# A decoder trunk on one core: GpSimd scales three pieces of the turned input, the compressed attention branch works on block-diagonal operands, and the split of the turned FFN hidden is placed later

## The chip, the cores and the metric

The kernel runs on one core of one Trainium2 chip. The metric is the device time of one execution in microseconds (us). The kernel before was timed three times: 1020.0, 1019.18 and 1019.8 us, median 1019.8 us. A separate execution was profiled.

## The reference

Two layers, each a half-step SwiGLU, a token mixer and another half-step SwiGLU; then a last norm. There are 256 rows of 1024 channels, the hidden width of the SwiGLU is 2816, and all is float32.

```python
for l in range(DEPTH):                       # 2
    x = x + 0.5 * swiglu(rms_norm(x, norm_ffn1[l]), gate1[l], up1[l], down1[l])
    x = x + hybrid_mixer(rms_norm(x, norm_mix[l]), w_in[l], ..., w_out[l])
    x = x + 0.5 * swiglu(rms_norm(x, norm_ffn2[l]), gate2[l], up2[l], down2[l])
return rms_norm(x, norm_final)

def swiglu(x, w_gate, w_up, w_down):
    return (silu(x @ w_gate) * (x @ w_up)) @ w_down
```

The mixer has four groups of four heads. Only one branch of one group matters here, the compressed branch of the sparse attention: keys and values of 256 rows are squeezed into 15 blocks each by a small network (`compress`), and each of the four query heads attends to the same 15 keys and values:

```python
kc, vc = compress(k_cmp, 0), compress(v_cmp, 1)          # 15 blocks x 64
s_cmp = einsum('bhtd,bnd->bhtn', q, kc) * scale - slopes * cmp_dist
p_cmp = masked_softmax(s_cmp, cmp_dist >= 0)
o_cmp = einsum('bhtn,bnd->bhtd', p_cmp, vc)              # times a gate, added to two other branches
```

## The kernel before, in words

**Halves and sets.** The 256 rows are two halves, h = 0 and h = 1, of 128 rows each. All large weights come as *sets* of 512 KB (`Set`, L123; a 128x2x512 tile). SyncE's queue loads a set into one of four `raw` buffers (L137); `split` (L119 to L121) then makes a high part `whi`, a copy on ScalarE, and a low part `wlo`, raw minus high, on VectorE. A product of set and half is six matmuls on TensorE (`Set.mm`, L149): two blocks of 128 rows, each high x high, high x low, low x high. The activations are split in the same way: `xhi` and `xlo` for the normed input, `hhi` and `hlo` for the hidden of the SwiGLU. Since all splits go through `split`, the trace books them under L115, the line in `keep` that issues them; the tile's name tells them apart.

**Order of the work.** The program walks over the sets (`consume`, L748): half 0 uses set i, half 1 uses set i - 5 (`LAG`), and loads run two sets ahead (`AHEAD`). After each use, `advance` (L179) moves all waiting jobs on by one step, so that a job which yields n is taken up again n uses later. No order is written out by hand beyond this: each engine runs its instructions in the order in which the framework has placed them. `tc.issue_after(ins)` places what is issued in it behind `ins`.

**The feed-forward blocks** (`add_ffn`, L281). There are four, each of 11 chunks of 256 hidden columns. A chunk is four gate/up sets (accumulator `ps_g`) and two down sets (`ps_d`); the down sets of chunk c stand behind the gate/up sets of chunk c + 2. Behind the last gate/up set, `gate_up` (L311) makes the hidden `sg` on ScalarE and VectorE (L318, L319). The hidden must be turned before the down product. In chunks 0, 1 and 10 TensorE does so (`turn`, L286). In the eight others (`turn_far`, L294), VectorE transposes 32x32 blocks (`z`, L298), GpSimd's queue writes them to DRAM in four pieces (`far<-z`, L301), reads them back four steps later (`pT<-far`, L305), and ten steps after that the split into `hhi` and `hlo` is issued (L309). Chunks 2 to 9 of a block are called far chunks below.

**The start** (`begin`, L717). The first block takes its input already turned from DRAM in four pieces: two for each half (`take_turned`, L237). VectorE multiplies each piece by the norm's weight `gcol` (L249), and the split follows. The first piece is cut in two parts of 128x256, the other three are 128x512. The order of the start is fixed by `keep` (L111), which puts every operation of VectorE and ScalarE behind the one before it. TensorE is kept busy by products with `idle`, a tile that VectorE zeroes (L96, L101).

**The compressed branch in the mixer.** `compress` (L482) loads the first layer's weights in four pieces into `raw` buffers and runs eight matmuls behind each (L497), so they stand between the products of the sets; the second layer gives `kc` (L517, the 64 x 15 keys, held twice in the 128 partitions) and `vc` (L519, 15 x 64). `cmp_branch` (L523) then uses `attend` (L429) as all branches do: four score products of a 64-row contraction (L399), a softmax (L402), a multiplication by the weight for each head (L437), four transposes (L445), a copy of 15x512 on ScalarE (L448), and four value products (L457), for each half and layer.

## Time and profile before

| | |
|---|---|
| three runs | 1020.0, 1019.18, 1019.8 us (median 1019.8) |
| the profiled execution's own time | 1020.97 us |
| its span, first to last instruction | 1019.2 us |
| granted TensorE clock, mean over the span | 0.995 |
| TensorE (PE) busy | 996.3 us, 98% |
| VectorE (DVE) busy | 642.0 us, 63% |
| ScalarE (ACT) busy | 515.8 us, 51% |
| GpSimd (POOL) busy | 195.0 us, 19% |
| mean DMA rate over the span | 197 GB/s |

A row of the timeline has the start of an operation, its duration and, in brackets, how long its engine stood idle before it and which event ended that. PE is TensorE, PEld its weight loads, which run beside its matmuls. TensorE's matmuls overlap: each 512-column product shows as some 0.39 us, though the next one starts earlier, so its pace is read from starts, not from durations. Idle time of an engine that nobody waits for costs nothing.

### The profile page before, as it was taken

The page shows a single profiled execution, that of the slowest core. Times are in us where ns is not written, and L with a number is a line of the kernel's source. Part 1 is how long each engine was busy: PE and PEld are TensorE (multiplying, and loading weights), DVE is VectorE, ACT ScalarE, POOL GpSimd, SP SyncE. Part 2 cuts the span into 40 slices and gives each one's busy share as a digit, 9 for nine tenths or more (in the row PEclk, how much of TensorE's full clock was granted, in tenths as well). Part 3 has the DMA queues.
Part 4 walks back from the last instruction along what each step waited for, and adds up shares of the span by engine and source line. Part 5 has one row for each costly group of instructions (what it writes and reads, how often), then busy time and mean ns, then how long its engine had stood idle before and what let it go on. Part 6 is the DMA issues. An engine that isn't in the chain of part 4 may idle for free.

```text
span 1019.2 us, 14178 instructions
## 1 busy us (share of the span) xinstructions
PE 996.3 (98%) x4899; PEld 801.4 (79%) x4899; DVE 642.0 (63%) x1223; ACT 515.8 (51%) x886; POOL 195.0 (19%) x351
## 2 busy tenths in 40 slices
PE   8999999999999999999999999999999999999997
PEld 5788787867778888788878888878678788888875
DVE  6565656786777456465755565648776775656464
ACT  6444444554665445354644454446466564445452
POOL 0132323010000023332102232310100001323230
PEclk9999999999999999999999999999999999999999
DMA  8677767644354466676656777755634455677671
GB/s 294 235 224 262 235 220 244 207 151 166 119 166 139 154 212 215 219 221 237 204 175 202 222 229 224 235 186 176 189 109 155 128 166 190 205 234 214 220 232 47
DMA packets 68855, 200.36 MB, mean 197 GB/s; under 512 B 12448, under 2 KB 20528, under 8 KB 68784
## 3 DMA queue, kind: packets, MB, share of 16 engines
q1 hardware_dynamic: 56352, 180.83, 55.1%
q0 software_dynamic: 11712, 17.86, 5.4%
q8 instruction: 38, 0.62, 0.3%
q10 hardware_dynamic: 720, 0.79, 0.2%
q14 instruction: 33, 0.27, 0.1%
HBM read 189.98 MB, written 9.45 MB: 196 GB/s over the span
## 4 chain that ended last, share of the span: by engine, by line
PE 40%; DMA 26%; DVE 11%; POOL 9%; issue 7%; ACT 7%; POOLq 0%; SPq 0%; ACTq 0%; DVEq 0%
PE ps_g L149 22%; DMA far<-z 13%; DMA pT<-far 11%; PE ps_d L149 10%; POOL far L301 9%; DVE wlo L115 5%; ACT whi L115 4%; PE ps_t L457 2%; DVE sg L319 2%; DMA wraw<-in_gu 1%; PE ps_t L445 1%; DVE z L298 1%; PE ps_d L399 1%; PE ps_t L379 1%; PE ps_t L262 1%
## 5 line engine op out<-in xcount | busy, mean ns | idle before, releaser
L115 DVE TENSOR_TENSOR wlo<-wraw,whi 128x1024 fp32r<-128x1024 f32 (+3 forms) x329 | 392.4, 1196 | 176.6 <-ACT whi L115 175.6
L115 ACT ACTIVATE whi<-wraw 128x1024 fp32r<-128x1024 f32 (+3 forms) x329 | 341.0, 1038 | 224.9 <-PE ps_g L149 105.4
L149 PE MATMUL ps_g<-whi,xhi 128*128 128x512 f32 (+2 forms) x896 | 352.0, 394 | 5.8 <-ACT whi L115 3.8
L149 PE MATMUL ps_g<-wlo,xhi 128*128 128x512 f32 (+2 forms) x896 | 347.5, 388 | 3.7 <-DVE wlo L115 3.6
L149 PE MATMUL ps_g<-whi,xlo 128*128 128x512 f32 (+2 forms) x896 | 346.4, 387 | 0.0
L149 PEld LDWEIGHTS ps_g<-whi,xhi 128*128 128x128 f32 x896 | 168.6, 188 | 47.5 <-ACT whi L115 6.7
L301 POOL DMA_DIRECT2D far<-z x256 | 139.8, 554 | 327.4 <-DVE z L298 322.8
L149 PEld LDWEIGHTS ps_g<-wlo,xhi 128*128 128x128 f32 x896 | 168.7, 188 | 37.3 <-DVE wlo L115 6.8
L149 PEld LDWEIGHTS ps_g<-whi,xlo 128*128 128x128 f32 x896 | 168.5, 188 | 31.7 <-DVE xlo L115 0.5
L149 PE MATMUL ps_d<-whi,hhi 128*128 128x512 f32 x352 | 138.9, 395 | 0.0
L149 PE MATMUL ps_d<-whi,hlo 128*128 128x512 f32 x352 | 137.8, 391 | 0.0
L149 PE MATMUL ps_d<-wlo,hhi 128*128 128x512 f32 x352 | 137.6, 391 | 0.0
L115 ACT ACTIVATE hhi<-pT 128x256 fp32r<-128x256 f32 x64 | 26.7, 417 | 153.4 <-DMA pT<-far 153.4
L115 DVE TENSOR_TENSOR hlo<-pT,hhi 128x256 fp32r<-128x256 f32 x64 | 27.2, 425 | 107.5 <-ACT hhi L115 107.4
L149 PEld LDWEIGHTS ps_d<-whi,hlo 128*128 128x128 f32 x352 | 66.4, 189 | 13.9
L149 PEld LDWEIGHTS ps_d<-wlo,hhi 128*128 128x128 f32 x352 | 66.6, 189 | 13.6
L149 PEld LDWEIGHTS ps_d<-whi,hhi 128*128 128x128 f32 x352 | 66.5, 189 | 13.4
L159 POOL TENSOR_TENSOR rstd<-ms,mhalf 128x1 f32<-128x1 f32 x14 | 8.6, 614 | 291.4 <-DVE ms L157 291.4
L305 POOL DMA_DIRECT2D pT<-far x64 | 35.6, 557 | 142.4 <-DMA far<-z 111.9
L318 ACT ACTIVATE sg<-ps_g,rstd 128x256 f32<-128x256 f32 x88 | 41.1, 467 | 22.4 <-PE ps_g L149 22.1
L319 DVE SCALAR_TENSOR_TENSOR sg<-ps_g,rstd,sg 128x256 f32<-128x256 f32 x88 | 42.1, 478 | 15.8 <-ACT sg L318 15.8
L416 ACT ACTIVATE p<-p,nm 128x128 f32<-128x128 f32 (+2 forms) x96 | 40.1, 419 | 22.8 <-DVE nm L408 10.5
(158 smaller groups left out, 654.4 us busy)
## 6 DMA issues: line engine op xcount, KB each, us to landing
wraw<-in_gu SPq DMA_DIRECT2D x175, 512.0 KB, 4.1
wraw<-in_down SPq DMA_DIRECT2D x88, 512.0 KB, 4.5
wraw<-in_win SPq DMA_DIRECT2D x24, 512.0 KB, 4.0
far<-z POOLq DMA_DIRECT2D x256, 32.0 KB, 4.0
pT<-far POOLq DMA_DIRECT2D x64, 128.0 KB, 3.7
wraw<-in_wout SPq DMA_DIRECT2D x16, 512.0 KB, 3.5
wraw<-in_win SPq DMA_DIRECT2D x16, 384.0 KB, 3.6
wraw<-in_w SPq DMA_DIRECT2D x8, 512.0 KB, 3.5
```

Source lines behind the costliest of these rows:

```text
L115: ins = f(*args, **kw)
L149: nc.tensor.matmul(acc, x_[k], w[:, k, :], start=first and i == 0, stop=last and i == 5)
L262: nc.tensor.transpose(pt[:, j, :], xg[:, j * P:(j + 1) * P], ident)
L298: nc.vector.transpose(st, hh)
L301: nc.gpsimd.dma_start(far[:, :, a_, :].rearrange("b j e -> j b e"), st[32 * a_:32 * a_ + 32].rearrange("j (b e) -> j b e", b=4))
L305: nc.gpsimd.dma_start(back, far.rearrange("b j a e -> (b j) (a e)"))
L318: nc.scalar.activation(sg, acc[h][:, :256], AF.Silu, scale=r)
L319: nc.vector.scalar_tensor_tensor(sg, acc[h][:, 256:], r, sg, op0=ALU.mult, op1=ALU.mult)
L379: nc.tensor.transpose(pt[:, j, :], z[:, j * P:(j + 1) * P], ident)
L399: nc.tensor.matmul(dst, qT[r, i // 2, :], keys(i)[r, :nk], start=True, stop=True)
L416: nc.scalar.activation(p[:, i, :], p[:, i, :], AF.Exp, bias=nm[:, i:i + 1], scale=-1.0, accum_out=den[:, i:i + 1])
L457: nc.tensor.matmul(o[64 * e:64 * e + 64, j, :], vals(2 * j + e, n), pts[n][:w, 2 * j + e, :], start=n == 0, stop=n == len(blocks) - 1)
```

## The change

In order of the program:

- A constant tile `pc` (128x4x32) is zeroed once on GpSimd; the warm-up products read the zeroed tile `ph` instead of `idle`, whose memset on VectorE goes.
- In `take_turned` the three 128x512 pieces are multiplied by `gcol` on GpSimd, outside the order that `keep` fixes; the two parts of the first piece stay on VectorE.
- `split` returns its ScalarE instruction, each set keeps its last one, and `turn_far` issues the split of the hidden behind the `whi` of the newest set loaded so far.
- `compress` loads its first layer's weights in two pairs and runs 16 matmuls behind each pair. `kc` becomes a block-diagonal tile (128x2x15) and `vc` a block-diagonal 128x256 in the buffer `blk`, both zeroed by GpSimd and filled by six small copies on VectorE.
- `cmp_branch` is written out: two score products of 128 rows x 30 columns, the softmax in `pc`, one multiplication for all heads, one transpose, a ScalarE copy of 128x128, and two value products.

```diff
@@ hybrid_kernel
+    pc = const.tile([P, 4, 32], F32, name="pc")
+    nc.gpsimd.memset(pc, 0.0)
...
-    idle = const.tile([P, P], mybir.dt.bfloat16, name="idle")
-    nc.vector.memset(idle, 0.0)
+    idle = ph.bitcast(mybir.dt.bfloat16)[:, :P]
@@ keep, split, Set.load
             fixed[engine] = ins
+        return ins
 
     def split(pt, hi, lo):
-        keep("ACT", nc.scalar.activation, hi, pt, AF.Copy)
+        first = keep("ACT", nc.scalar.activation, hi, pt, AF.Copy)
         keep("DVE", nc.vector.tensor_tensor, lo, pt, hi.bitcast(F32), op=ALU.subtract)
+        return first
...
-                split(r[:, k], self.hi[:, k], self.lo[:, k])
+                self.last = split(r[:, k], self.hi[:, k], self.lo[:, k])
@@ take_turned
-                keep("DVE", nc.vector.tensor_tensor, xg[:, k], xg[:, k], g, op=ALU.mult)
+                if parts > 1:
+                    keep("DVE", nc.vector.tensor_tensor, xg[:, k], xg[:, k], g, op=ALU.mult)
+                else:
+                    nc.gpsimd.tensor_tensor(xg[:, k], xg[:, k], g, op=ALU.mult)
                 split(xg[:, k], hi[:, k], lo[:, k])
@@ turn_far
             hT[h, c] = tuple(hbuf.tile([P, 2, P], F32R, name=f"h{t}{h}") for t in ("hi", "lo"))
-            split(back, *(t.rearrange("p k (a i) -> p k a i", a=4) for t in hT[h, c]))
+            with tc.issue_after(sets[done[0] - 1].last.ins):
+                split(back, *(t.rearrange("p k (a i) -> p k a i", a=4) for t in hT[h, c]))
@@ compress
-            for q in range(4):
-                w1 = raw.tile([P, 2, 512], F32, name="wraw").rearrange("p j (c e) -> p j c e", e=P)
-                nc.sync.dma_start(w1, a["w1"][l, q])
-                yield 2
-                for j in range(2):
-                    for c in range(4):
-                        nc.tensor.matmul(part[32 * c:32 * c + NB, :P], blk[:, c // 2, 8 * (c % 2) + 2 * q + j, :],
-                                         w1[:, j, c, :], start=q == 0 and j == 0, stop=q == 3 and j == 1)
+            for qs in ((0, 1), (2, 3)):
+                w1 = []
+                for q in qs:
+                    w1.append(raw.tile([P, 2, 512], F32, name="wraw").rearrange("p j (c e) -> p j c e", e=P))
+                    nc.sync.dma_start(w1[-1], a["w1"][l, q])
+                    yield 2
+                for q in qs:
+                    for j in range(2):
+                        for c in range(4):
+                            nc.tensor.matmul(part[32 * c:32 * c + NB, :P], blk[:, c // 2, 8 * (c % 2) + 2 * q + j, :],
+                                             w1[q % 2][:, j, c, :], start=q == 0 and j == 0, stop=q == 3 and j == 1)
...
-            kc = small.tile([P, NB], F32, name="kc", bufs=1)
-            nc.vector.tensor_copy(kc, cp[:, :NB])
-            M["vc"] = small.tile([NB, 64], F32, name="vc", bufs=1)
-            nc.vector.tensor_copy(M["vc"], cp[:NB, 64:128])
+            kc = small.tile([P, 2, NB], F32, name="kc", bufs=1)
+            nc.gpsimd.memset(kc, 0.0)
+            M["vc"] = work.tile([P, 2, 16, NB], F32, name="blk", bufs=1).rearrange("p a b c -> p (a b c)")[:, :256]
+            nc.gpsimd.memset(M["vc"], 0.0)
+            for e in range(2):
+                r = slice(64 * e, 64 * e + 64)
+                nc.vector.tensor_copy(kc[r, e, :], cp[r, :NB])
+            for i in range(4):
+                c = 128 * (i // 2) + 64 * (i % 2)
+                nc.vector.tensor_copy(M["vc"][32 * i:32 * i + NB, c:c + 64], cp[:NB, 64:128])
@@ cmp_branch
-            yield from attend(h, lambda: M["nq", h], lambda i: M["kc"], lambda i: tbl["cmp"][:, h, i, :],
-                              lambda i, n: M["vc"], put_part(h, False, True), NB, f"d{h}", gate=0, guard=True)
+            s = bank(f"d{h}")[:, :4 * NB].rearrange("p (j e k) -> p j e k", j=2, e=2)
+            for j in range(2):
+                nc.tensor.matmul(s[:, j].rearrange("p e k -> p (e k)"), M["nq", h][:, j, :],
+                                 M["kc"].rearrange("p e k -> p (e k)"), start=True, stop=True)
+            p, rd = softmax(h, [s[:, :, e, :] for e in range(2)], lambda i: tbl["cmp"][:, h, i, :], NB,
+                            guard=True, p=pc[:, :, :NB])
+            w = small.tile([P, 4], F32, name="gw")
+            nc.vector.tensor_tensor(w, rd, M["gate", h][:, 0::3], op=ALU.mult)
+            nc.vector.tensor_tensor(p, p, w.unsqueeze(2).to_broadcast([P, 4, NB]), op=ALU.mult)
+            yield 3 + 2 * h
+            yield 0
+            pt = bank("t")
+            nc.tensor.transpose(pt[:, :P], pc.rearrange("p i k -> p (i k)"), ident)
+            sb = work.tile([P, 4, P], F32, name="pT")[:, 0, :]
+            nc.scalar.activation(sb, pt[:, :P], AF.Copy)
+            yield 2
+            o = bank("t")[:, :256].rearrange("p (j t) -> p j t", j=2)
+            for j in range(2):
+                nc.tensor.matmul(o[:, j, :], M["vc"][:, P * j:P * j + P], sb, start=True, stop=True)
+            put_part(h, False, True)(o)
```

**Where the instructions move.** ScalarE in the first feed-forward block, before (`hhi_694` is half 1 of one far chunk, `hhi_704` half 0 of the next, `sg` the hidden of a later one):

```order
L115 ACTIVATE whi<-wraw 128x1024 x3
L115 ACTIVATE hhi_694<-pT 128x256
L115 ACTIVATE whi<-wraw 128x1024
L115 ACTIVATE hhi_704<-pT 128x256
L115 ACTIVATE whi<-wraw 128x1024
L318 ACTIVATE sg<-ps_g,rstd 128x256
L115 ACTIVATE whi<-wraw 128x1024
L318 ACTIVATE sg<-ps_g,rstd 128x256
```

and with the change:

```order
L116 ACTIVATE whi<-wraw 128x1024 x5
L325 ACTIVATE sg<-ps_g,rstd 128x256
L116 ACTIVATE whi<-wraw 128x1024
L116 ACTIVATE hhi_694<-pT 128x256
L325 ACTIVATE sg<-ps_g,rstd 128x256
L116 ACTIVATE hhi_704<-pT 128x256
L116 ACTIVATE whi<-wraw 128x1024 x5
```

Five of the six `whi` of a chunk now stand in one run behind the second `hhi`. `hhi_694` has moved behind three `whi` and the first `sg` that stood after it, `hhi_704` behind two `whi` and both `sg`. VectorE at the end of the first feed-forward block, before (`hlo_1712` is half 1 of chunk 9, the last far chunk; L278 is the residual, first of columns 0 to 511 and then of columns 512 to 1023 of half 0):

```order
L115 TENSOR_TENSOR hlo_1712<-pT,hhi_1711 128x256
L115 TENSOR_TENSOR wlo<-wraw,whi 128x1024
L115 TENSOR_TENSOR wlo<-wraw,whi 128x2x400
L278 SCALAR_TENSOR_TENSOR x_84<-ps_d_422,x_84 128x512
L228 TENSOR_TENSOR xn<-x_84,gain 128x512
L319 SCALAR_TENSOR_TENSOR sg<-ps_g,rstd,sg 128x256
L115 TENSOR_TENSOR wlo<-wraw,whi 128x2x400
L115 TENSOR_TENSOR xlo_1678<-ps_t,xhi_1677 128x512
L278 SCALAR_TENSOR_TENSOR x_84<-ps_d_446,x_84 128x512
```

and with the change:

```order
L116 TENSOR_TENSOR wlo<-wraw,whi 128x2x400
L284 SCALAR_TENSOR_TENSOR x_84<-ps_d_422,x_84 128x512
L231 TENSOR_TENSOR xn<-x_84,gain 128x512
L326 SCALAR_TENSOR_TENSOR sg<-ps_g,rstd,sg 128x256
L116 TENSOR_TENSOR wlo<-wraw,whi 128x2x400
L116 TENSOR_TENSOR xlo_1678<-ps_t,xhi_1677 128x512
L284 SCALAR_TENSOR_TENSOR x_84<-ps_d_446,x_84 128x512
L116 TENSOR_TENSOR hlo_1712<-pT,hhi_1711 128x256
```

`hlo_1712` has moved from ahead of both residuals of half 0 to behind the second. TensorE in the first mixer, at the scores of the compressed branch of half 0, before:

```order
L149 MATMUL ps_g<-wlo,xhi_1796 128x512
L399 MATMUL ps_d_2374<-kc,qT 128x15
L399 MATMUL ps_d_2375<-kc,qT 128x15
L399 MATMUL ps_d_2374<-kc,qT 128x15
L399 MATMUL ps_d_2375<-kc,qT 128x15
L149 MATMUL ps_g<-whi,xlo_1797 128x512
L379 MATMUL ps_t<-ident,z 128x128 x2
```

and with the change:

```order
L152 MATMUL ps_g<-wlo,xhi_1796 128x512
L152 MATMUL ps_g<-whi,xlo_1797 128x512
L547 MATMUL ps_d_2380<-kc,qT 128x30 x2
L386 MATMUL ps_t<-ident,z 128x128 x2
L406 MATMUL ps_d_2443<-kT_win,qT 128x256
```

Four products have become two, and they stand next to other small products instead of between two products of a set. SyncE's queue keeps its order. GpSimd's gets eight operations more: before the first `rstd` two memsets and the three multiplications, and in each mixer the memset of `blk` (in the second one that of `kc` too) behind the second half's addition L571.


## Rows read from the trace of the kernel before

**Rows 1.** The profile's page of the whole execution: busy time of each engine with its share of the span and its instructions, TensorE (PE) first; and of the list of DMA issues the read-back of the turned hidden: its count, size and median time in us from issue to landing.

```profile
PE 996.3 (98%) x4899; PEld 801.4 (79%) x4899; DVE 642.0 (63%) x1223; ACT 515.8 (51%) x886; POOL 195.0 (19%) x351
...
pT<-far POOLq DMA_DIRECT2D x64, 128.0 KB, 3.7
```

**Rows 2.** The waits of TensorE over the whole span: engine, line and tile that waited, what ended the wait, us in total, times, longest.

```profile
PE ps_g L149 <- ACT whi L115: 3.8, 4, 2.0
PE ps_g L149 <- DVE wlo L115: 3.6, 6, 0.8
...
PE ps_t L457 <- ACT pT L448: 0.9, 2, 0.5
```

**Rows 3.** Seven stretches of 12 us, TensorE alone: the stretch, its length, busy us and instructions that ran in it, granted clock, share of the DMA engines, GB/s. Six hold the longest idle times of ScalarE before `hhi`, one in each; 130 to 142 us is a stretch of the first feed-forward block without any.

```profile
93.00:105.00 12.00, 11.84 (x53) 1.00 0.71 247
112.00:124.00 12.00, 11.56 (x51) 1.00 0.66 227
163.00:175.00 12.00, 11.06 (x49) 1.00 0.59 213
410.00:422.00 12.00, 10.50 (x45) 1.00 0.48 156
664.00:676.00 12.00, 10.31 (x38) 0.86 0.52 173
960.00:972.00 12.00, 11.23 (x48) 1.00 0.52 171
130.00:142.00 12.00, 12.00 (x55) 1.00 0.61 190
```

**Rows 4.** The waits of ScalarE (ACT) over the whole span, columns as in rows 2.

```profile
ACT hhi L115 <- DMA pT<-far: 153.4, 59, 6.6
```

**Rows 5.** The timeline of 664 to 676 us, all engines in order of start: start, us, engine, line, operation, tile written and read, shapes, and in brackets the idle time of that engine before it and what ended it.

```profile
665.07 0.56 POOL L305 DMA_DIRECT2D pT<-far  x1 [1.32 <-DMA far<-z]
...
667.74 0.39 PE L149 MATMUL ps_g<-wlo,xhi 128*128 128x512 f32 x1
...
667.87 0.42 ACT L115 ACTIVATE hhi<-pT 128x256 fp32r<-128x256 f32 x1 [6.58 <-DMA pT<-far]
667.97 0.39 PE L149 MATMUL ps_g<-whi,xlo 128*128 128x512 f32 x1
668.20 1.04 ACT L115 ACTIVATE whi<-wraw 128x1024 fp32r<-128x1024 f32 x1
...
669.29 0.50 PE L149 MATMUL ps_g<-whi,xhi 128*128 128x512 f32 x1 [0.93 <-ACT whi L115]
...
670.40 0.45 ACT L318 ACTIVATE sg<-ps_g,rstd 128x256 f32<-128x256 f32 x1
...
670.55 0.51 PE L149 MATMUL ps_g<-wlo,xhi 128*128 128x512 f32 x1 [0.76 <-DVE wlo L115]
...
672.37 0.63 PE L149 MATMUL ps_d<-wlo,hhi 128*128 128x512 f32 x1
...
672.80 0.63 PE L149 MATMUL ps_d<-whi,hlo 128*128 128x512 f32 x1
```

**Rows 6.** The timeline of 182 to 193 us, the end of the first feed-forward block: VectorE's (DVE's) second residual of the first half, and the first product that reads `hlo` of the second half's chunk 9.

```profile
189.97 0.68 DVE L278 SCALAR_TENSOR_TENSOR x<-ps_d,x 128x512 f32<-128x512 f32 x1
...
192.45 0.39 PE L149 MATMUL ps_d<-whi,hlo 128*128 128x512 f32 x1
```

**Rows 7.** The timeline of 222.5 to 225 us, in the first mixer: GpSimd's (POOL's) addition of two 128x512 operands, and two small operations of VectorE, one that begins while it runs and one after it.

```profile
222.87 1.36 POOL L571 TENSOR_TENSOR foxt<-foxt,tbl_tri 128x512 f32<-128x512 f32 x1 [4.83 <-DMA foxt<-line]
...
223.16 1.09 DVE L543 TENSOR_TENSOR lsq<-lsw 128x4 f32<-128x4 f32 x1
...
224.38 0.16 DVE L545 TENSOR_SCALAR lsp<-lsq 128x4 f32<-128x4 f32 x1
```

**Rows 8.** The timeline of the start: the multiplication of the first turned piece that the change moves, and the split and the product behind it; and, 18 us later, a split that waited for its weights.

```profile
8.94 0.68 DVE L115 TENSOR_TENSOR xn<-xn,gcol 128x512 f32<-128x512 f32 x1
...
9.66 0.63 ACT L115 ACTIVATE xhi<-xn 128x512 fp32r<-128x512 f32 x1 [1.36 <-DVE xn L115]
...
10.34 1.22 PE L149 MATMUL ps_g<-whi,xhi 128*128 128x512 f32 x2 [0.38 <-ACT xhi L115]
...
28.32 1.06 ACT L115 ACTIVATE whi<-wraw 128x1024 fp32r<-128x1024 f32 x1 [1.76 <-DMA wraw<-in_gu]
```

**Rows 9.** TensorE's timeline of 229 to 260 us, in the first mixer: a burst of the first layer of the compression (L497, each matrix product shows as two records), the scores (L399), the turned weights (L445) and the value product (L457) of the compressed branch of the first half, and for three of these runs the weight-set product that comes next.

```profile
229.96 0.63 PE L497 MATMUL ps_d<-wraw,blk 128*15 128x128 f32 x16
230.52 0.50 PE L149 MATMUL ps_g<-whi,xhi 128*128 128x512 f32 x1
...
248.39 0.62 PE L399 MATMUL ps_d<-kc,qT 64*128 64x15 f32 x8
248.94 0.50 PE L149 MATMUL ps_g<-whi,xlo 128*128 128x512 f32 x1
...
254.42 0.61 PE L445 MATMUL ps_t<-ident,p 128*15 128x128 f32 x4
254.79 0.47 PE L149 MATMUL ps_g<-whi,xhi 128*128 128x512 f32 x1
...
258.84 0.65 PE L457 MATMUL ps_t<-pT,vc 15*64 15x128 f32 x8
259.42 0.50 PE L149 MATMUL ps_g<-whi,xhi 128*128 128x512 f32 x1
```

More of the change, by code (lines that the diff above doesn't have):

```diff
@@ L400, in scores, with softmax @@
             return views
-        def softmax(h, views, table, nk, sink=None, guard=False):
-            p = work.tile([P, 4, P * (h + 1)], F32, name=f"p{h}")[:, :, :nk]
+        def softmax(h, views, table, nk, sink=None, guard=False, p=None):
+            if p is None:
+                p = work.tile([P, 4, P * (h + 1)], F32, name=f"p{h}")[:, :, :nk]
             nm = small.tile([P, 4], F32, name="nm")
```

## The prediction

> **What bounds the kernel now.** I read, in this order, the page, TensorE's waits, equal stretches of TensorE, ScalarE's waits, and the timeline at the worst place. TensorE is busy for 996.3 us, 98% of the span, with 4899 matmuls; VectorE for 63%, ScalarE for 51%, GpSimd for 19% [rows 1]. So the time is TensorE's matmuls plus the places where it stands still. Those I looked for in its waits. By name they are small: 3.8 us for `whi`, 3.6 us for `wlo`, nothing else over 2 us [rows 2]. But "busy" hides part of it, because matmuls overlap and an operation that starts late still shows its full duration. I therefore counted matmuls in equal stretches. In 12 us of an undisturbed feed-forward stretch 55 run; in six other stretches 53, 51, 49, 45, 38 and 48, which is 284 where 330 would fit [rows 3]. At the pace of undisturbed products, 0.227 us from start to start (667.74 to 667.97 in [rows 5], rounded there to 0.23), the 46 missing ones are 46 x 0.227 = 10.4 us. That is the largest loss I found.
>
> What stands behind it is ScalarE's own wait. It stood idle 153.4 us in 59 waits before `hhi`, for the DMA `pT<-far` [rows 4]: 2.6 us each. ScalarE executes in order, so the next `whi` stood behind. [rows 5] shows the worst of them. ScalarE idled 6.58 us until the turned hidden landed, began `hhi` at 667.87, and the `whi` behind it at 668.20. TensorE had finished its sets with the product at 667.97 and got the next only at 669.29; then it waited once more, for `wlo`, until 670.55. After that its products start 0.43 us apart instead of 0.227 (672.37 to 672.80), which is the lower clock level of 1.2 GHz; the granted clock of that stretch is 0.86, that of the others 1.00, or 2.4 GHz [rows 3]. ScalarE works ahead of TensorE by up to two sets (`AHEAD`). Only the six longest of the 59 waits, those of [rows 3], used up that lead, and they cost the 10.4 us.
>
> **The change, part by part.**
>
> *The split behind the newest `whi`.* The order of ScalarE moves the first of each pair of `hhi` behind three `whi` and one `sg`: 3 x 1.04 + 0.45 = 3.6 us of work [rows 5]. ScalarE does this work in time that was idle. Does the data arrive by then? In [rows 5] the first `hhi` began when its data landed, at 667.87; the read-back for the second was issued at 665.07, and with the median 3.7 us from issue to landing [rows 1] it is there at 668.8. The `sg` that now comes first began at 670.40, after TensorE had stood still for 1.09 us (668.20 to 669.29) and 1.03 us (669.52 to 670.55); without these it can begin at 668.3. The first `hhi` in its new place then begins at 668.3 + 0.45 + 1.04 = 669.8, and the second one `hhi` and one `sg` later. Both find their data there, with 1 to 2 us to spare, at the worst of the six places. Should a wait be left, ScalarE meets it just after the newest `whi`, with its whole lead of two sets, 24 x 0.227 = 5.4 us, ahead of TensorE. Is `h` needed sooner? Its down sets stand 12 sets behind the chunk's hidden, and FAR + BACK = 14 steps at two per set are 7 sets: five sets are left, 5 x 12 x 0.227 = 13.6 us, against a delay of 3.6 us. It costs nothing. I take 9.5 of the 10.4 us, since each count of [rows 3] can be off by a matmul at the edges; bounds 7 and 10.4. **-9.5 us.**
>
> *The multiplications on GpSimd.* On VectorE one of 128x512 took 0.68 us [rows 8]. The nearest row for GpSimd is an addition of two 128x512 operands, 1.36 us [rows 7]. The first moved one waited for no DMA at 8.94; it stood behind VectorE's other work. GpSimd is empty and can begin as soon as the piece has landed; `xhi` then starts earlier by at most its 1.36 us idle time, or 0.6 us later if the piece had only just landed. TensorE lost 0.38 us there. The two other pieces are needed by later sets. Beyond that the start is a supply problem: 18 us later `whi` waits 1.76 us for its weights [rows 8], and what TensorE gained before is handed back there. I take -0.3 us, with bounds -1.0 and +1.5 (the rival below). The memset of `idle` that goes is hidden behind the first weights' load. **-0.3 us.**
>
> *The compressed branch.* Small products cost by run, not by column. A burst of eight first-layer matmuls takes 230.52 - 229.96 = 0.56 us and the product behind it starts late; two bursts are joined twice per layer, and each saves one entry and exit, which I put at 0.2 us (the product behind a burst lasts 0.50 instead of 0.39, and the burst begins some 0.1 us late): 4 x 0.2 = 0.8 us. The scores take 248.94 - 248.39 = 0.55 us for four products (eight records), the transposes 254.79 - 254.42 = 0.37 us for four, the value products 259.42 - 258.84 = 0.58 us for four [rows 9]. Two products, one transpose and two products in their place, with the run's own entry unchanged, save about 0.3, 0.2 and 0.1 us: 0.6 us for each half and layer, four times, 2.4 us. **Sum -3.2 us.** Bounds: -5, if the waits for ScalarE's copy before the value products (0.9 us, [rows 2]) and half of the runs' entries go too; +1, if the six copies that fill `kc` and `vc` and the shared `pc` make each score wait a quarter of a microsecond.
>
> A rule of the Trainium skill speaks against this part. The row shows 0.55 us for four score products of 64 rows, eight records [rows 9], 0.07 us per record. "TensorEngine Tiling (Array Packing)", section "When to Use Tiling", advises two row tiles where the contraction is 64 or less, and "Key Properties" says that tiles work independently, in parallel. By it the four old products already ran as two, and a pair of 128-row products with half zeros would save nothing: without the 0.3 us, the sum would be 1.2 us higher. Nothing in the rest depends on these sentences.
>
> *At the end of a block* the last far chunk's `hlo` now stands behind the second residual of the first half. That one began at 189.97 and lasted 0.68; 0.42 us for `hlo` makes 191.1, and TensorE first reads it at 192.45 [rows 6]. 1.35 us are left. Costs nothing, but the cover is thin.
>
> **Sum.** -9.5 - 0.3 - 3.2 = -13.0 us. The profiled execution's own time is 1020.97 us, 1.17 above the median of the runs. 1020.97 - 13.0 = 1008.0; against the median 1019.8 - 13.0 = **1006.8 us**, which I forecast.
>
> **The rivals.**
>
> *The wait only moves.* ScalarE still meets the DMA late in some chunks, now with an `sg` and five `whi` behind it. For it: 153.4 us is much to lose, and the landing times vary by several us between chunks. Against it: the spare time and the full lead worked out above. If half of the 10.4 us stayed, the term would be 5.2 instead of 9.5, and the time 1006.8 + 4.3 = 1011.1.
>
> *The mixer gives nothing and the start gives back.* The compressed branch's small products stand in a stretch where other small work (transposes, other heads) already separates the sets' products, and VectorE gets six copies in place of two. With 0 instead of -3.2 that is 1010.0. The start can add to it by a lock, and the trace shows one: VectorE's `lsq` of 128x4 began at 223.16 while GpSimd's addition ran (222.87 to 224.23) and lasted 1.09 us, to 224.25; the small operation after it took 0.16 us [rows 7]. If each of the three multiplications holds VectorE back in this way, its `wlo` and `xlo` of the start come up to 1.36 us later each time, less the 0.68 us that VectorE no longer spends: 3 x 0.68 = 2 us, of which TensorE would feel 1.5 at most, since VectorE also waits there for ScalarE. Then 1010.0 + 0.3 + 1.5 = 1011.8. The Trainium skill, "SBUF — State Buffer", section "SBUF: two separate sides", has this as a rule: VectorE with two operands in SBUF and a GpSimd operation that reads SBUF take one shared port pair in turn, each for its whole instruction. By that rule, the trace agrees, with 1.09 us for the small operation.
>
> *Slower: the later split holds the `pT` buffers.* There are two, and the read-back of the next far chunk into one waits for the `hlo` that read it before. If the split is late, the next read-back is issued later, the split behind it later still, and ScalarE stands in every far chunk. It decides when the wait at the new place exceeds the lead of 5.4 us: then each of the 32 far chunks loses the rest. 0.5 us in each, 16 us in all, are more than the 13 us of the forecast: 1006.8 + 16 = 1022.8, slower. Against it: a chunk is 6 sets x 12 x 0.227 = 16.3 us, and delay 3.6 plus landing 4 leave half of it free [rows 1, 5].
>
> *The change doesn't move what matters.* The placement "behind the newest `whi`" could come to the old place where few sets are loaded. The order shows that it does not in the chunks that I compared; but the six losses may have a second cause (the weights' own DMA: the six stretches move 156 to 247 GB/s, the undisturbed one 190 [rows 3]). Then only the mixer counts: 1019.8 - 3.2 = 1016.6.
>
> **How the numbers follow.** My forecast has 0.62, the first rival 0.12, the second 0.16, the slower one 0.04, the last 0.06. The range takes in the first two rivals and the bounds: at the lower end 10.4 + 1.0 + 5 = 16.4 below the median, 1003.4; at the upper end the first rival together with a mixer at +1 would be 1015, which is too unlikely, so I stop at 1013. About 0.2% of the time, 2 us, is what a measurement can tell from no change. All cases but the slower one and a part of the last lie below 1017.8: faster 0.92, same 0.04, slower 0.04.
>
> **What would show it.** Right: ScalarE's wait before `hhi` falls from 153 us to a third or less, stretches at the six places hold 54 or 55 matmuls per 12 us, and no stretch in a feed-forward block has a granted clock below 1.00. TensorE's waits for `whi` and `wlo` keep little beyond the 2.0 us of the start. In the mixers the scores' run takes 0.3 us or less, and each mixer is 1.6 us shorter. VectorE's operations at 9 to 14 us show durations above 1.3 us only if the lock bites. Wrong: if the six places keep their losses, the first term is wrong; if VectorE's `hlo` at the end of a block starts after the product that reads it would have, the thin cover was too thin; if the mixers are as long as before, the run cost of small products is not what I took it for.

## The result, and the profile after

The changed kernel took 1003.91 us in the median of three runs (1003.59, 1003.91, 1004.93), the kernel before 1019.8 us: a ratio of 0.9848, 95% interval 0.9825 to 0.987, which is 13.3 to 17.8 us less. On another chip, four runs gave 1004.49 us and a ratio of 0.9852 (0.9832 to 0.9872). The forecast was 1006.8 us, and the result lies only 0.5 us above the lower end of its range, 1003.4. The profiled execution after took 1003.59 us, its span is 1001.4.

The page of the changed kernel: busy times as in [rows 1], and the chain of work that ended last, by engine; then that chain of the kernel before.

```profile
PE 985.8 (98%) x4855; PEld 800.4 (80%) x4855; DVE 641.6 (64%) x1215; ACT 515.4 (51%) x886; POOL 200.3 (20%) x359
...
PE 91%; DVE 5%; ACT 3%; DMA 1%; issue 1%; POOLq 0%; SPq 0%; ACTq 0%; DVEq 0%
```

```profile
PE 40%; DMA 26%; DVE 11%; POOL 9%; issue 7%; ACT 7%; POOLq 0%; SPq 0%; ACTq 0%; DVEq 0%
```

TensorE is busy 10.5 us less, but only a part of that is work taken away; late matmuls also count as busy. The chain now runs through TensorE for 91% of its length; before it was 40%, with 26% for DMAs, `far<-z` and `pT<-far` almost alone. TensorE's waits over the span, as in [rows 2]:

```profile
PE ps_g L152 <- ACT whi L116: 2.7, 2, 1.5
PE ps_t L453 <- DVE lsp L585: 2.1, 2, 1.1
...
```

The wait for `whi` is down to 2.7 us, the one for `wlo` is no longer listed. What `hhi` waited for, 153.4 us in [rows 4], has gone altogether. In ScalarE's waits the DMA `pT<-far` no longer occurs. Three rows of them, one that has grown and the two longest with `hhi`:

```profile
ACT whi L116 <- DMA wraw<-in_win: 12.0, 6, 3.4
...
ACT whi L116 <- ACT hhi L116: 10.7, 28, 0.6
...
ACT hhi L116 <- PE ps_t L296: 8.6, 7, 2.4
```

`whi` waits behind an `hhi` 28 times, for 0.6 us at most, and `hhi` itself waits only for TensorE, in the chunks that never used the DMA. The row that has grown is the first, 12.0 us for weights of the mixer's input projection, 2.1 us before; it comes back below. The six stretches of [rows 3], each moved by what the kernel had gained by then:

```profile
90.00:102.00 12.00, 12.00 (x55) 1.00 0.81 283
108.00:120.00 12.00, 12.00 (x54) 1.00 0.74 250
158.00:170.00 12.00, 12.00 (x56) 1.00 0.79 239
403.00:415.00 12.00, 12.00 (x55) 1.00 0.73 227
652.00:664.00 12.00, 12.00 (x56) 1.00 0.78 256
944.00:956.00 12.00, 12.00 (x55) 1.00 0.74 254
```

54 to 56 matmuls stand in each where there were 38 to 53, and the clock is 1.00 in all. The worst place, that of [rows 5]:

```profile
654.46 0.55 POOL L311 DMA_DIRECT2D pT<-far  x1 [2.53 <-DMA far<-z]
...
658.42 0.48 ACT L325 ACTIVATE sg<-ps_g,rstd 128x256 f32<-128x256 f32 x1 [1.66 <-PE ps_g L152]
...
658.79 1.05 ACT L116 ACTIVATE whi<-wraw 128x1024 fp32r<-128x1024 f32 x1
...
659.74 0.40 ACT L116 ACTIVATE hhi<-pT 128x256 fp32r<-128x256 f32 x1
...
660.04 0.46 ACT L325 ACTIVATE sg<-ps_g,rstd 128x256 f32<-128x256 f32 x1
...
660.40 0.41 ACT L116 ACTIVATE hhi<-pT 128x256 fp32r<-128x256 f32 x1
```

The read-back of the second `hhi` was issued at 654.46. ScalarE reached the first `hhi` at 659.74 and the second at 660.40, and found the data there both times (no bracket). The second is used 5.9 us after its read-back was issued, where the median landing takes 3.9 us in this execution.

Read from the starts of the same matmuls in both traces, the 17.7 us between the two profiled executions fall as follows. By 40 us the changed kernel is ahead by 2.6. The six places give 0.5, 0.73, 1.49, 2.07, 3.85 and 1.35, together 10.0. The two mixers, from the first product of the input projection to the first of the output projection, give 1.2 and 1.9. The other 2.0 us are steps at the ends and starts of feed-forward blocks, 1.4 of them between 495 and 520 us, where the third block follows on the second. These go with the split's place as well: a step of 1.1 to 1.5 us of TensorE stands there in all five traces taken with the old place or with the tie two sets earlier (below), and in none of the nine with the tie behind the newest set.

### The profile page after: what moved, and what is told of

Its sections match the earlier page's. It is cut to its first block, busy times and chain, and to the rows that moved or that the text cites. A ratio compares the mean times of both kernels' runs of the same rounds, so it can differ in the third digit from the quotient of the medians.

```text
span 1001.4 us, 14096 instructions
## 1 busy us (share of the span) xinstructions
PE 985.8 (98%) x4855; PEld 800.4 (80%) x4855; DVE 641.6 (64%) x1215; ACT 515.4 (51%) x886; POOL 200.3 (20%) x359
## 4 chain that ended last, share of the span: by engine, by line
PE 91%; DVE 5%; ACT 3%; DMA 1%; issue 1%; POOLq 0%; SPq 0%; ACTq 0%; DVEq 0%
PE ps_g L152 56%; PE ps_d L152 27%; PE ps_t L465 1%; DVE wlo L116 1%; PE ps_t L453 1%; PE ps_d L406 1%; PE ps_t L386 1%; PE ps_t L268 1%; ACT p L424 1%; ACT whi L116 1%; PE ps_t L406 1%; PE ps_t L296 1%; DMA wraw<-in_gu 0%; DMA wraw<-in_win 0%; DVE blk L496 0%
## 5 line engine op out<-in xcount | busy, mean ns | idle before, releaser
L152 PEld LDWEIGHTS ps_d<-whi,hhi 128*128 128x128 f32 x352 | 66.1, 188 | 13.3
L424 ACT ACTIVATE p<-p,nm 128x128 f32<-128x128 f32 (+1 forms) x80 | 35.5, 445 | 19.7 <-DVE nm L420 10.3
L304 DVE STREAM_TRANSPOSE z<-sg 128x256 f32<-128x256 f32 x64 | 28.4, 443 | 1.2
L156 ACT ACTIVATE sq<-x 128x512 bf16<-128x512 f32 (+1 forms) x29 | 17.6, 607 | 17.5 <-DVE x L284 17.4
```

Of the source, the lines that this page charges most:

```text
L152: nc.tensor.matmul(acc, x_[k], w[:, k, :], start=first and i == 0, stop=last and i == 5)
L156: nc.scalar.activation(sq[:, :sl.stop - sl.start], x[h][:, sl], AF.Square, scale=1.0 / 32.0, accum_out=stat)
L304: nc.vector.transpose(st, hh)
L424: nc.scalar.activation(p[:, i, :], p[:, i, :], AF.Exp, bias=nm[:, i:i + 1], scale=-1.0, accum_out=den[:, i:i + 1])
```

## The experiments

All times are medians on the chip of that run; kernels in one list shared the chip and the runs of the kernel before. "Matmuls by 40 us" are the counts of the stretch 0 to 40 us in the traces.

**Each part alone**, on the kernel before, which took 1020.96 us in 25 runs here.

*The split tied, alone.* The edit is the `issue_after` line in `turn_far` with what it needs.

```diff
-            split(back, *(t.rearrange("p k (a i) -> p k a i", a=4) for t in hT[h, c]))
+            with tc.issue_after(sets[done[0] - 1].last.ins):
+                split(back, *(t.rearrange("p k (a i) -> p k a i", a=4) for t in hT[h, c]))
```

> The kernel before with only the split of the turned hidden tied behind the newest whi. Theory (the wait before hhi stood in front of whi, and the six longest waits used up the lead): every one of the six steps goes and nothing else changes: 10 us less, 1009.5 to 1010, with ScalarE's wait for pT near zero and the start and the mixers as before. Rival (part of the gain in the feed-forward blocks comes from the earlier start or from the shorter mixers, which shift the phase between DMA and ScalarE): less than 7 us, 1013 or more.

Measured: 1009.19 us, ratio 0.9889 (0.9865 to 0.9913), which is 8.9 to 13.8 us less. TensorE's waits for the two parts of the weights:

```profile
PE ps_g L151 <- ACT whi L115: 1.9, 2, 1.5
...
PE ps_g L151 <- DVE wlo L115: 0.2, 1, 0.2
```

No `pT<-far` is left in ScalarE's waits. The theory holds, and the rival falls: neither the start nor the mixers are needed for it. With it falls the prediction's last rival, a second cause of the six losses: nothing but the place of the split was changed here, and the steps are gone. A second thing shows only in the runs. The kernel before spread over 1016.9 to 1027.5 us here; the four runs with the tie lie within 1008.88 to 1009.77. The losses that went were also those that changed from run to run: in the traces of the three kernels below, which keep the old place of the split, the steps stand at partly different chunks (at 166, 412, 480 and 667 us in one, at 84, 101, 118, 169 and others in the next).

*The multiplications on GpSimd, alone.*

```diff
-                keep("DVE", nc.vector.tensor_tensor, xg[:, k], xg[:, k], g, op=ALU.mult)
+                if parts > 1:
+                    keep("DVE", nc.vector.tensor_tensor, xg[:, k], xg[:, k], g, op=ALU.mult)
+                else:
+                    nc.gpsimd.tensor_tensor(xg[:, k], xg[:, k], g, op=ALU.mult)
```

> The kernel before with only the three multiplications on GpSimd. Theory now (the start gains because ScalarE and VectorE split the next sets earlier, so that TensorE's waits at 17, 22 and 30 us go): 2.0 to 2.6 us less, 1017.2 to 1017.8, all of it by 35 us. The prediction's theory (the loads bind again at 30 us): 0 to 0.5 us less. Lock theory (VectorE held back by GpSimd): up to 1.5 us more.

Measured: 1017.53 us, ratio 0.997 (0.9948 to 0.9991), with runs from 1015.3 to 1021.97. The interval, 0.9 to 5.3 us less, holds the theory's 2.0 to 2.6 and leaves out the other two, the prediction's 0 to 0.5 only narrowly. With the old place of the split the runs spread too far to size the start; that was taken up again below.

*The compressed branch, alone*, with bursts of eight as before and the warm-up products on `ph`.

```diff
-            kc = small.tile([P, NB], F32, name="kc", bufs=1)
+            kc = small.tile([P, 2, NB], F32, name="kc", bufs=1)
...
-            yield from attend(h, lambda: M["nq", h], lambda i: M["kc"], lambda i: tbl["cmp"][:, h, i, :],
...
+            for j in range(2):
+                nc.tensor.matmul(s[:, j].rearrange("p e k -> p (e k)"), M["nq", h][:, j, :],
+                                 M["kc"].rearrange("p e k -> p (e k)"), start=True, stop=True)
...
```

> The kernel before with only the compressed branch in block-diagonal form (and the warm-up on the zeroed ph), first-layer bursts of eight as before. Prediction's theory (run cost of small products): 2.4 us less, 0.6 for each half and layer, 1017.4. Rival by tiling (the old 64-row products ran side by side, so half of the array's work is only moved): 1.2 us less, 1018.6. Rival by waits (six copies and two memsets before kc and vc are there): no gain or up to 1 us more.

Measured: 1017.3 us, ratio 0.9973 (0.9951 to 0.9994). In its trace the two mixers are 4.2 us shorter (97.31 and 97.69 us before, 95.42 and 95.36 now), more than the 2.4 expected. The time alone, 0.6 to 5.0 us less, does not tell the theory's 2.4 from the tiling rival's 1.2; the trace, with more than either, speaks for the theory. Its mixers are not exact to better than 0.7 us: in the traces of the two kernels above, which leave the mixers as they were, they are 0.7 and 0.3 us longer than before. Of the rivals by waits, one sign is there and small: TensorE waits 0.5 us in two pieces for the weights in `pc`.

*The pairs, alone.*

```diff
-            for q in range(4):
+            for qs in ((0, 1), (2, 3)):
...
+                for q in qs:
...
```

> The kernel before with only the first layer of the compression in two bursts of 16 matmuls instead of four of eight. Theory: 0.2 us for each burst that is joined, four in all: 0.8 us less, 1019.0. Rival (two raw buffers held at once delay the weight loads behind them): 1 us more or worse, with a wait for whi in the mixer.

Measured: 1020.34 us, ratio 0.9994 (0.9971 to 1.0018), from 3.0 us less to 1.8 more, so the time decides nothing. In its trace the mixers are 2.6 us longer (99.55 and 98.06), and ScalarE waits 11.3 us for weights of the input projection, 2.1 before. This is what the rival said.

**Undoing parts of the changed kernel**, on one chip, where the kernel before took 1019.5 us. First the changed kernel again.

> The changed kernel again, on the chip that the next three share. Every theory: 1003.9 as before, and its runs within 1 us or so of each other, since the waits that moved from run to run (the landing of pT) are gone, where the kernel before spreads over several us.

Measured: 1004.49 us (1003.25 to 1005.68), the base of this list. The runs spread over 2.4 us, more than the 1 us expected.

*Back to VectorE.*

```diff
-                if parts > 1:
...
-                    nc.gpsimd.tensor_tensor(xg[:, k], xg[:, k], g, op=ALU.mult)
+                keep("DVE", nc.vector.tensor_tensor, xg[:, k], xg[:, k], g, op=ALU.mult)
```

> The changed kernel with the three multiplications back on VectorE, in the fixed order of the start. Reading of the two traces (2.6 us gained by 35 us): 1006.5. Reading corrected by the other runs, whose start was also 0.7 to 1.3 us earlier than in the profiled run of before without any change to it: 1005.0 to 1005.5. Prediction (0.3 us, handed back at 30 us): 1004.2.

Measured: 1007.06 us (1004.5 to 1007.5), 2.6 us more than the base. TensorE by 40 us, in the first trace of the changed kernel, in this one and in the kernel before (the columns of [rows 3]):

```profile
0.00:40.00 40.00, 36.25 (x147) 0.96 0.86 293
```

```profile
0.00:40.00 40.00, 35.46 (x135) 0.96 0.83 286
```

```profile
0.00:40.00 40.00, 35.60 (x135) 0.96 0.83 288
```

These are 147 matmuls against 135 and 135. Over all traces taken but the last, which has no multiplications, the five with the multiplications on VectorE have 135 to 141 by 40 us (mean 137.6), the eight with GpSimd 142 to 152 (mean 147.6). Ten matmuls at 0.227 are 2.3 us, and the two groups don't overlap. The prediction's 0.3 us falls, and so do its bound of 1.0 us less and the sentence that the gain would be handed back to the loads.

*The pairs undone.*

```diff
-            for qs in ((0, 1), (2, 3)):
...
+            for q in range(4):
...
```

> The changed kernel with the first layer's weights of the compression again in four pieces and four bursts of eight matmuls. Prediction's theory (0.2 us for each joined burst): 0.8 us slower, 1004.7. Theory from the two single changes (the branch alone shortens the mixers by 4.2 us, the pairs alone lengthen them by 2.6 and both together shorten them by 3.1): 1 us faster, 1002.9, the first mixer shortened most.

Measured: 1002.62 us (1001.79 to 1004.14), 1.9 us less than the base. The runs overlap, and on the third chip below the same kernel took 1003.86 us, so the time says only that the pairs do not gain; what they cost is read from the traces. ScalarE's wait for the weights in the mixers, 12.0 us above, here:

```profile
ACT whi L116 <- DMA wraw<-in_win: 1.8, 2, 1.1
```

In the second trace of the changed kernel, the base of this list, such a wait reaches TensorE; the first trace lists no wait of TensorE for `z`. The timeline of the first mixer in the second trace:

```profile
232.82 1.06 ACT L116 ACTIVATE whi<-wraw 128x1024 fp32r<-128x1024 f32 x1 [3.66 <-DMA wraw<-in_win]
...
233.61 1.26 POOL L608 TENSOR_TENSOR foxt<-foxt,tbl_tri 128x512 f32<-128x512 f32 x1 [6.10 <-DMA foxt<-line]
...
233.78 0.46 ACT L398 ACTIVATE z<-ps_g,rq 128x256 f32<-128x256 f32 x1
...
233.91 2.04 DVE L116 TENSOR_TENSOR wlo<-wraw,whi 128x1024 fp32r<-128x1024 f32 x1 [2.31 <-ACT whi L116]
...
234.29 0.44 PE L386 MATMUL ps_t<-ident,z 128*128 128x128 f32 x2 [0.89 <-ACT z L398]
```

`whi` waits 3.66 us for its weights, `z` stands behind it on ScalarE, and TensorE waits 0.89 us for `z`, and a little later 0.86 more for the keys of the next branch. A pair holds two of the four `raw` buffers until its 16 matmuls have run, so a set behind it is loaded late. A second effect comes on top. The late `wlo` runs beside GpSimd's second addition and takes 2.04 us, where one without company takes 1.23, and the keys stand behind it on VectorE. In all ten mixers traced with pairs a `wlo` of 128x1024 meets that addition, and takes 1.44 to 2.04 us; in the eighteen traced without, only two do, at 1.26 and 1.39. How the cost divides between the late load and this meeting, no run here separates. How much reaches TensorE changes from run to run: the mixers of the changed kernel were 3.1 us shorter than before in one trace and 1.1 in the other, and 2.6 and 3.2 in the two other edits of it that keep the pairs; in the traces without pairs that have the new branch (leaving aside the edit that holds the addition back by its data) 3.4 to 4.2.

*The addition held back.* TensorE's longest waits in the mixers are for `lsp`, the log-sigmoid chain of VectorE, in which one small operation takes 1.1 to 1.2 us beside GpSimd's first addition, as in [rows 7].

```diff
-            nc.vector.scalar_tensor_tensor(M["lf", h], q, -2.0, m0, op0=ALU.mult, op1=ALU.add)
+            M["end", h] = nc.vector.scalar_tensor_tensor(M["lf", h], q, -2.0, m0, op0=ALU.mult, op1=ALU.add)
...
-            nc.gpsimd.tensor_tensor(t[:, :, 2 * h, :], t[:, :, 1 + h, :],
...
+            while ("end", 1) not in M:
+                yield 1
+            with tc.issue_after(M["end", 1].ins):
+                nc.gpsimd.tensor_tensor(t[:, :, 2 * h, :], t[:, :, 1 + h, :],
...
```

> The changed kernel with GpSimd's addition of the first half of the forgetting attention's table held back until the second half's log-sigmoid chain on VectorE has ended. Lock theory (that addition, 1.38 us, holds up the chain's small operation by 1.1 us, and TensorE waits 1.1 us for the chain in each layer): the 1.2 us operation shrinks to 0.15 us, TensorE's wait for lsp falls from 2.1 us to nearly nothing, 2 us less: 1001.9. Rival (the wait is for the transposed weights' multiplications behind the chain, or is taken over by the next late thing): 0 to 0.5 us less.

Measured: 1003.52 us (1003.27 to 1005.25). The addition still began in the middle of the chain, so the edit did not do what it was meant to.

```profile
217.36 1.32 POOL L611 TENSOR_TENSOR foxt<-foxt,tbl_tri 128x512 f32<-128x512 f32 x1 [4.62 <-DMA foxt<-line]
...
217.61 1.09 DVE L580 TENSOR_TENSOR lsq<-lsw 128x4 f32<-128x4 f32 x1
```

`tc.issue_after` on an instruction of VectorE did not make GpSimd wait for it here. The run says nothing for or against the lock, and the question is put again below.

**On the kernel without pairs**, on a third chip, where the kernel before took 1019.32 us.

> The changed kernel without the pairs again, the base for the next three on the same chip: 1002.6 as before.

Measured: 1003.86 us (1002.12 to 1004.78), ratio 0.9845 (0.9831 to 0.9859). That is 1.2 us more than the same kernel took on the chip before, and hardly less than the changed kernel with its pairs (ratios 0.9848 and 0.9852).

*The addition behind the chain, by its data.*

```diff
-            nc.gpsimd.tensor_tensor(t[:, :, 2 * h, :], t[:, :, 1 + h, :],
...
+            while ("lf", 1) not in M:
+                yield 1
+            gate = nullcontext()
+            if h == 0:
+                seen = small.tile([P, 4], F32, name="seen", bufs=1)
+                gate = tc.issue_after(nc.gpsimd.tensor_tensor(seen, M["lf", 1], M["lf", 1], op=ALU.add).ins)
+            with gate:
+                nc.gpsimd.tensor_tensor(t[:, :, 2 * h, :], t[:, :, 1 + h, :],
...
```

> As the base, and GpSimd's first addition in each mixer (1.38 us) is put behind a small GpSimd operation that reads the result of VectorE's log-sigmoid chain, so that it can't run while the chain runs. Lock theory: the 1.1 to 1.2 us operation of the chain shrinks to 0.15 us, TensorE's wait for lsp (1.5 us in two waits) nearly goes: 1 to 2 us less, 1000.6 to 1001.6. Rival (the wait is handed on to what follows the chain, or the small operation isn't held by GpSimd at all): within 0.5 us of the base; in the second case the small operation keeps its 1.1 us.

Measured: 1001.05 us (1000.45 to 1001.98), ratio 0.982 (0.9808 to 0.9833), 2.8 us less than its base, where 1 to 2 were expected. The runs do not overlap. The base: GpSimd's addition, the chain's operation `lsw` of 128x4, and TensorE's wait for the chain.

```profile
215.76 1.31 POOL L605 TENSOR_TENSOR foxt<-foxt,tbl_tri 128x512 f32<-128x512 f32 x1 [3.81 <-DMA foxt<-line]
215.88 1.21 DVE L575 TENSOR_TENSOR lsw<-lse,lsr 128x4 f32<-128x4 f32 x1
...
221.17 0.30 PE L453 MATMUL ps_t<-ident,p 128*128 128x128 f32 x1 [0.65 <-DVE lsp L582]
```

With the edit: the same operation, then the small one on GpSimd that waits for the chain, then the addition.

```profile
217.35 0.14 DVE L575 TENSOR_TENSOR lsw<-lse,lsr 128x4 f32<-128x4 f32 x1
...
221.87 0.20 POOL L610 TENSOR_TENSOR seen<-lf 128x4 f32<-128x4 f32 x1 [9.62 <-DVE lf L586]
222.02 1.29 POOL L612 TENSOR_TENSOR foxt<-foxt,tbl_tri 128x512 f32<-128x512 f32 x1
```

`lsw` takes 0.14 us instead of 1.21, TensorE's wait for `lsp` is no longer listed, and in the traces each mixer has gained 1.05 us at this place. That the small operation was held up by the addition is shown, and so is that TensorE waited for it. Two mixers make 2.1 of the 2.8 us; the rest is within the spread of the runs. The addition now meets a `wlo` of 128x1024, which takes 1.60 us instead of 1.23 in both mixers, but no wait of TensorE for it is listed. All runs of this version lie below all runs of both kernels, though those of the changed kernel were on other chips.

*The tie two sets earlier.*

```diff
-            with tc.issue_after(sets[done[0] - 1].last.ins):
+            with tc.issue_after(sets[done[0] - 3].last.ins):
```

> As the base, but the split of the turned hidden is tied behind the whi of the set before the last two instead of the newest: both hhi then stand before two whi that have not been made. Theory (a wait costs what goes beyond ScalarE's lead): the typical late landing, some 2 us, stays hidden, the latest ones (3.7 to 5 us late) do not: 1 to 6 us slower than the base, ScalarE's wait before hhi back at 100 us or more, the loss in steps at a few places of the feed-forward blocks. Rival (any distance between the split and its old place does): within 0.5 us of the base.

Measured: 1021.03 us (1013.26 to 1022.66), as slow as the kernel before (ratio 1.0001, 0.998 to 1.0021), 17 us above its base. The direction is right, the rival is out, and the size is far off the 1 to 6 us expected. The profiled execution took 1015.61 us, one of the fastest of the twelve. In it ScalarE waits less before `hhi` than in [rows 4]:

```profile
ACT hhi L116 <- DMA pT<-far: 94.0, 52, 4.2
```

but shorter waits cost. Here is the longest, 4.21 us, with what follows:

```profile
978.98 0.42 ACT L116 ACTIVATE hhi<-pT 128x256 fp32r<-128x256 f32 x1 [4.21 <-DMA pT<-far]
...
979.31 1.04 ACT L116 ACTIVATE whi<-wraw 128x1024 fp32r<-128x1024 f32 x1
...
979.92 0.39 PE L152 MATMUL ps_d<-whi,hlo 128*128 128x512 f32 x1
...
980.40 0.50 PE L152 MATMUL ps_d<-whi,hhi 128*128 128x512 f32 x1
...
981.66 0.50 PE L152 MATMUL ps_d<-wlo,hhi 128*128 128x512 f32 x1 [0.76 <-DVE wlo L116]
```

`whi` begins at 979.31, TensorE has run out by 979.92 + 0.23 and starts the next product at 980.40, the one for `wlo` at 981.66. In this trace waits of 3.2 to 3.5 us already make steps; in the trace before, nothing under 4.7 us did. Both `hhi` stand ahead of two `whi` that are still to be made, so the lead is spent when ScalarE gets there. The expectation had counted the lead of the steady rhythm, as if those two were there.

*No multiplication at all.*

```diff
-                else:
-                    nc.gpsimd.tensor_tensor(xg[:, k], xg[:, k], g, op=ALU.mult)
```

> As the base, but the three pieces are not multiplied by the weight at all, which leaves out a part of the first norm. It is the bound for the start. Theory (VectorE's 0.7 us operations that took 1.52 us beside GpSimd are not waited for by TensorE): 0 to 0.5 us faster than the base. Lock theory (the two held-up operations and GpSimd's own 1.73 us are on TensorE's path): 1 to 2 us faster.

Measured: 1002.53 us (1001.88 to 1003.36), 1.3 us less than the base, with overlapping runs. This kernel leaves out a part of the first norm, so it is only a bound. In the trace it has 144 matmuls by 40 us, fewer than the base's 152. Whether the lock costs anything in the start stays open: the time speaks for some 1.3 us, the trace for nothing.

## Why the prediction was right, point by point

**The split: 9.5 us predicted, 10.0 at the six places, 11.3 (8.9 to 13.8) for the tie alone.** Right in mechanism and size. That ScalarE's wait for `pT` disappears, that the six places hold 54 or more matmuls, and that the clock stays at 2.4 GHz there, all came as said. The tie alone gave more than the 10.4 us that were there to win at the six places. The place where the third block follows on the second adds to them, and the prediction had put the end of a block at nothing; by which wait the tie helps there was not tested. Besides, the losses vary from run to run, and the profiled execution before was one draw of them.

**The multiplications: 0.3 predicted, 2.3 measured.** This is the term that was wrong, beyond its bound of 1.0, by the sentence "what TensorE gained before is handed back there". I had read one wait of `whi` for its weights at 28.32 [rows 8] as a limit of the memory. The runs show that the gain is kept. With the multiplications on VectorE, `xhi` waits 1.9 us for `z`, and ScalarE waits 4.2 us in five pieces for weights in the first 36 us; in the first trace of the changed kernel it is 0.2 us for `z`, 1.0 for the piece after it and one piece of 2.0 for weights. Undoing it brings the waits back (1.9, and 4.8 in five pieces). By which way the gain comes is not shown. A load starts when `wlo` frees a buffer, so earlier splits could bring earlier loads; but that link was not tested by itself, and the kernel without any multiplication also waits for weights, 4.0 us in five pieces, with 144 matmuls by 40 us.

**The lock in the start** was there, as its rival said. In the first trace of the changed kernel two `xlo` of 128x512 took 1.52 us beside GpSimd and a third 0.68 after it, and GpSimd's third multiplication took 1.73 instead of 1.04 beside VectorE.

```profile
7.62 1.04 POOL L255 TENSOR_TENSOR xn<-xn,gcol 128x512 f32<-128x512 f32 x1 [6.48 <-DMA xn<-in_xT]
...
9.34 1.10 POOL L255 TENSOR_TENSOR z<-z,gcol 128x512 f32<-128x512 f32 x1 [0.68 <-DMA z<-in_xT]
9.46 1.52 DVE L116 TENSOR_TENSOR xlo<-xn,xhi 128x512 fp32r<-128x512 f32 x1
...
11.29 1.73 POOL L255 TENSOR_TENSOR pT<-pT,gcol 128x512 f32<-128x512 f32 x1 [0.86 <-DMA pT<-in_xT]
...
12.04 1.52 DVE L116 TENSOR_TENSOR xlo<-z,xhi 128x512 fp32r<-128x512 f32 x1
...
14.63 0.68 DVE L116 TENSOR_TENSOR xlo<-pT,xhi 128x512 fp32r<-128x512 f32 x1
```

The Trainium skill ("SBUF — State Buffer", "SBUF: two separate sides") calls the shared port pair an exclusive lock, which whoever starts first holds for the whole instruction. With this rule the trace agrees in both directions. But at 9 to 14 us no wait of TensorE for `xlo` is listed; the rival's 1.5 us more did not come, and what the lock costs here is bounded only by the experiment without multiplications.

**The mixers: 3.2 predicted, 3.1 in one trace and 1.1 in another.** The sum was near by luck; both terms were off. The prediction's sign, each mixer 1.6 us shorter, came as 1.2 and 1.9 in the first trace, and as 0.5 longer and 1.6 shorter in the second. In the changed kernel's first mixer, the runs of [rows 9]:

```profile
224.71 1.07 PE L508 MATMUL ps_d<-wraw,blk 128*15 128x128 f32 x32
225.71 0.50 PE L152 MATMUL ps_g<-whi,xhi 128*128 128x512 f32 x1
...
243.31 0.53 PE L547 MATMUL ps_d<-kc,qT 128*128 128x30 f32 x4
243.67 0.41 PE L386 MATMUL ps_t<-ident,z 128*128 128x128 f32 x2
...
249.84 0.30 PE L557 MATMUL ps_t<-ident,pc 128*128 128x128 f32 x1
249.89 0.47 PE L152 MATMUL ps_g<-whi,xlo 128*128 128x512 f32 x1
...
253.39 0.61 PE L563 MATMUL ps_t<-pT,blk 128*128 128x128 f32 x4
253.75 0.48 PE L152 MATMUL ps_g<-whi,xhi 128*128 128x512 f32 x1
```

From its first product to the next matrix product behind it, the run of the scores takes 0.36 us (0.55 before, and not the 0.3 or less of the prediction), the one transpose 0.05 (0.37), the value products 0.36 (0.58). That saves 0.73 us in this half and layer where I had 0.6, and the branch alone gave 4.2 us by the trace. A burst of 16 takes 1.00 us where two of eight took 1.12, so a joined pair saves 0.12 and not 0.2. What the pairs cost by their longer hold on `raw` I had not counted at all: with the saving taken off, 1.3 us by the means of the traces (2.5 us gained in the four with pairs, 3.8 in the five without). The rule of the Trainium skill on row tiling ("TensorEngine Tiling (Array Packing)", "When to Use Tiling"), two row tiles for a contraction of 64, would have left the scores at 0.55 us, as the prediction read it. The run got shorter by a third, so here two products of 128 rows were quicker than four of 64. The places are not quite alike: behind the new scores comes a transpose, behind the old ones came a set product.

**The rivals.** The wait did not move elsewhere. The later split does not hold up the read-backs so far that ScalarE feels it: no wait for `pT<-far` is left. `hlo` at the end of the block ended at 185.71 with its first reader at 187.15: 1.4 us to spare, as worked out.

## What to carry to other kernels

An in-order engine that makes one stream ahead of its reader and also waits for a slow transfer should meet that transfer right behind the newest item of the stream, where its lead is full; here the same wait two items earlier cost all that was gained. Count items per equal stretch to find such losses, since busy time and the waits by name showed half of them. Before merging small bursts, ask what they hold: a buffer held twice as long can cost more than the saved entry, by late loads and by what the late work then meets.

## What the runs showed of the hardware

VectorE's operations of 128x4 took 1.1 to 1.3 us instead of 0.14 to 0.16 while a GpSimd operation of two 128x512 operands ran, and large ones were held up too (`wlo` 2.04 us instead of 1.23, and `xlo` 1.52 instead of 0.68 beside a multiplication). GpSimd's multiplication beside VectorE took 1.73 instead of 1.04. The first I had seen before the change; that it was worth 1.05 us of TensorE's time in each mixer, I had not expected. Run-to-run spread can be a symptom of such a wait: 6.7 to 10.6 us in the kernels that were run 10 to 25 times with the old place of the split or the tie two sets earlier, 0.9 to 3.0 us in the four or five runs of each kernel with the tie behind the newest set. Few runs understate a spread: the first three of the kernel before lay within 0.8 us. The fairer figure is 2.4 us over twelve runs, those of the changed kernel and of the edit that left the addition where it was.
